# One of three sums of weight blocks moved from VectorE into an accumulating DMA

## The chip, the cores and the metric

The kernel runs on one core of a Trainium2 chip. The metric is the device time of one execution in microseconds; for the kernel before it is the median of three runs.

## The reference, cut to what matters

Two layers, each with a half-step SwiGLU feed-forward block, a parallel token mixer and a second feed-forward block, on 256 tokens of 1024 features. The change touches only the feed-forward blocks:

```python
def _swiglu(h, wg, wu, wd):
    return (jax.nn.silu(h @ wg) * (h @ wu)) @ wd

for l in range(DEPTH):
    f = _swiglu(_rmsnorm(h, ff1_norm_pre[l]), ff1_w_gate[l], ff1_w_up[l], ff1_w_down[l])
    h = h + 0.5 * _rmsnorm(f, ff1_norm_post[l])
    m = _hybrid_mixer(_rmsnorm(h, mix_norm_pre[l]), w_in[l], ...)
    h = h + _rmsnorm(m, mix_norm_post[l])
    f = _swiglu(_rmsnorm(h, ff2_norm_pre[l]), ff2_w_gate[l], ff2_w_up[l], ff2_w_down[l])
    h = h + 0.5 * _rmsnorm(f, ff2_norm_post[l])
```

`wg` and `wu` are 1024 by 2816, `wd` is 2816 by 1024, all float32.

## The kernel before, in words

**Precision.** Each float32 operand is split into two float32r parts: ScalarE copies it into `hi` (line 98 for weights, 199 for activations) and VectorE subtracts to get `lo` (line 99, 200). A product is three matmuls: hi by hi, hi by lo, lo by hi.

**Stages.** There are four feed-forward stages, two mixers between them. In a feed-forward stage the 2816 hidden columns are eleven units of 256. Units 0 and 1 are done first (`ffn_first`, line 307). Then come, in turn, "quads" of two units (blocks 2, 5 and 8, each two units wide) and "pairs" of one unit (4, 7, 10; lines 285 to 287). After each, the down projections of the units before it are added into PSUM accumulators (`mm_rows`, line 322), once for each half of the tokens; in the code such a pair of projections is a `downs` entry.

**A quad** multiplies the 256 by 1024 activations by the 1024 by 512 columns of the gate and of the up weights in one two-by-two block product with seven products in place of eight (Winograd's form of Strassen's). The right factors are the four weight blocks g1, u1, g2, u2 and their sums:

- T1 = g1 + u1
- T2 = g1 + u1 + u2
- T3 = u1 + u2
- T4 = g1 + u1 + u2 + g2

Each factor is 128 partitions by 2048 elements and is used by one product (`product`, line 416: 12 matmuls of 512 columns); four of the factors are sums. The left factors S1 to S4 and X11, X12, X22 are made once for each stage in `pre_turn`. The function `ffn_quad` multiplies T1, g1, T2, T3, g2, T4 and u2 in this order, with the sums of the products on VectorE between them.

**The weight pipeline** (`Weights`). `plan_ffn` lists units (one load of 1 MB each, issued by SyncE, line 77) and jobs (one split each). Four raw buffers hold loaded units; a job frees those it names. Five pairs of split buffers hold `hi` and `lo` until the product that uses them is done. A job can name a sum: VectorE then adds two raw buffers into the job's own raw buffer in two halves (line 97) ahead of the split. `pump` loads and splits as far ahead as the buffers let it.

**What sets the order.** The code gives each instruction a place; a list scheduler at build time may move an instruction ahead of others on its engine when its inputs and its buffer would be ready earlier by the scheduler's own times. On the chip each engine then runs its list in order. So splits, left factors and down projections are interleaved in another order than the code has them.

**GpSimd** has only the power -0.5 of the norms to compute (line 210). Temporary activations of 512 elements live in tag `t`, which has 22 buffers; the mixers use most of them.

Of the kernel before, what the change touches and what calls it, by code (L numbers as in the profile page):

```python
# [13 lines left out]
AF = mybir.ActivationFunctionType  # L14
ALU = mybir.AluOpType
AX = mybir.AxisListType

P = 128
# [10 lines left out]
UNIT = 2048  # L29
# [18 lines left out]
class Weights:  # L48
# [9 lines left out]
        self.units.append((src, cols))  # L58
        return len(self.units) - 1

    def job(self, unit, sum_of=None, free=(), pieces=2):


        self.jobs.append((unit, sum_of, free, pieces))
        return len(self.jobs) - 1

    def plan(self, src, cols=UNIT, pieces=2):
# [17 lines left out]

    def split_next(self):
        i, nc = self.split, self.nc
        u, sum_of, free, pieces = self.jobs[i]
        cols, raw = self.units[u][1], self.raw[u]
        hi = self.splitp.tile([P, KD * QDT], F32R, tag="hi", name=f"hi{i}")  # L90
        lo = self.splitp.tile([P, KD * QDT], F32R, tag="lo", name=f"lo{i}")
        step = cols // pieces
        for c in range(0, cols, step):
            s = slice(c, c + step)
            if sum_of:
                x, op, y = sum_of
                nc.vector.tensor_tensor(raw[:, s], self.raw[x][:, s], self.raw[y][:, s], op=op)  # L97
            nc.scalar.activation(hi[:, s], raw[:, s], AF.Copy)  # L98
            nc.vector.tensor_tensor(lo[:, s], raw[:, s], hi[:, s].bitcast(F32), op=ALU.subtract)  # L99
        for v in free:  # L100
            del self.raw[v]
            self.live -= 1
        self.parts[i] = (hi, lo)
        self.split += 1
        self.held += 1
# [25 lines left out]
def hybrid_trunk_kernel(ctx: ExitStack, tc: tile.TileContext, a, out: bass.AP):  # L131
    nc = tc.nc
# [3 lines left out]
    tmp = ctx.enter_context(tc.tile_pool(name="tmp", bufs=1))  # L136
# [3 lines left out]
    ids = iter(range(10**6))  # L140

    def buf(dtype=F32, n=512, tag="t"):
        return tmp.tile([P, n], dtype, tag=tag, name=f"{tag}{next(ids)}", bufs={"t": 22, "n": 8}[tag])

    def tiny(n):
        return small.tile([P, n], F32, tag=f"s{n}", name=f"s{next(ids)}", bufs=2 if n > 64 else 12)
# [1 line left out]
    def bank(tag="wk"):  # L148
        return psum.tile([P, 512], F32, tag=tag, name=f"{tag}{next(ids)}")
# [4 lines left out]
    W = Weights(nc, rawp, splitp)  # L154
# [20 lines left out]
    ones = tmp.tile([1, P], F32, tag="n", name="ones", bufs=8)  # L175
    nc.vector.memset(ones, 1.0)
    zeros = buf(BF16, 512, "n")
    nc.vector.memset(zeros, 0.0)
    warm = bank()
# [33 lines left out]
    def square_sum(x, n, gain=1.0):  # L213

        junk, ssq = buf(BF16, 512, "n"), tiny(1)
        nc.scalar.activation(junk, x, AF.Square, scale=1.0 / (gain * math.sqrt(n)), accum_out=ssq)  # L216
        return ssq

    def post(t, f, gain, store=None):

        fg = [buf(tag="n"), buf(tag="n")]

        def scaled(i):
            nc.vector.tensor_tensor(fg[i], f[i], gains[:, 1, i * 512 : (i + 1) * 512], op=ALU.mult)

        ssq = [square_sum(f[0], D, gain)]
        scaled(0)
        ssq.append(square_sum(f[1], D, gain))
        r = rsqrt_sum(ssq, EPS / (gain * gain))
        scaled(1)  # L230
        for i in range(2):
            s = slice(i * 512, (i + 1) * 512)
            nc.vector.scalar_tensor_tensor(h[:, t, s], fg[i], r, h[:, t, s], op0=ALU.mult, op1=ALU.add)
            if store:
                store(t, s)
# [90 lines left out]
    def plan_ffn(l, n):  # L326


        p = {}

        def down(i):
            p["d", i] = W.plan(a[f"ff{n}_d"][l, i])

        def pair(i):
            for k in "gu":
                p[k, i] = W.plan(a[f"ff{n}_{k}"][l, PAIRS.index(i)])

        for i in range(2):
            for k in range(2):
                p["f", i, k] = W.plan(a[f"ff{n}_f"][l, 2 * i + k], pieces=4)  # L340
        before = list(FIRST)
        for i in range(2, NU):
            if i in PAIRS:
                pair(i)
                for b in before:
                    down(b)
                before = [i]
            elif i in QUADS:
                src = a[f"ff{n}_q"][l, QUADS.index(i)]
                g1, u1, u2 = (W.unit(src[k]) for k in (0, 1, 3))  # L350
                p["T1", i] = W.job(u1, (g1, ALU.add, u1))
                p["g1", i] = W.job(g1)
                p["T2", i] = W.job(u1, (u1, ALU.add, u2))
                p["T3", i] = W.job(g1, (u1, ALU.subtract, g1), free=(g1,))
                late = i == QUADS[-1]
                if not late:
                    down(before[0])
                g2 = W.unit(src[2])
                p["g2", i] = W.job(g2)
                for b in before[1:]:  # L360
                    down(b)
                p["T4", i] = W.job(u1, (u1, ALU.add, g2), free=(u1, g2))
                p["u2", i] = W.job(u2, free=(u2,))
                if late:
                    down(before[0])
                before = [i, i + 1]
        for b in before:
            down(b)
        return p
# [40 lines left out]
    def product(ps, left, job, first):  # L410

        hi, lo = (w[:, :UNIT].rearrange("p (k n) -> p k n", k=4) for w in W.get(job))
        parts = [(k, i) for k in range(4) for i in range(2)] + [(k, 2) for k in range(4)]
        for n, (k, i) in enumerate(parts):
            x, w = ((left[0], hi), (left[0], lo), (left[1], hi))[i]
            nc.tensor.matmul(ps, x[:, k, :], w[:, k, :], start=first and n == 0, stop=n == len(parts) - 1,  # L416
                             skip_group_check=not first)
        W.done(job)

    def ffn_quad(i, p, left, turn, downs):  # L420


        late = i == QUADS[-1]
        turn(0)
        pc = bank()
        product(pc, left["S1"], p["T1", i], True)
        h1 = buf()
        nc.scalar.activation(h1, pc, AF.Copy)
        pa = bank()
        product(pa, left["X11"], p["g1", i], True)  # L430
        w2 = buf()
        nc.scalar.activation(w2, pa, AF.Copy)
        turn(1)
        W.pump()
        pb = bank()
        product(pb, left["S2"], p["T2", i], True)
        nc.vector.tensor_tensor(w2, pb, w2, op=ALU.add)
        nc.vector.tensor_tensor(pc, pc, w2, op=ALU.subtract)  # L438
        W.pump()
        pd = bank()  # L440
        product(pd, left["S3"], p["T3", i], True)
        nc.vector.tensor_tensor(pd, pd, w2, op=ALU.add)
        nc.vector.tensor_tensor(h1, h1, pd, op=ALU.subtract)
        W.pump()
        if not late:
            downs[0]()
        product(pa, left["X12"], p["g2", i], False)
        h0 = buf()
        nc.scalar.activation(h0, pa, AF.Silu)
        W.pump()  # L450
        for f in downs[1:]:
            f()
        product(pd, left["X22"], p["T4", i], False)
        nc.scalar.activation(w2, pd, AF.Silu)
        nc.vector.tensor_tensor(h1, h1, w2, op=ALU.mult)
        W.pump()
        product(pc, left["S4"], p["u2", i], False)
        nc.vector.tensor_tensor(h0, pc, h0, op=ALU.mult)
        W.pump()
        if late:  # L460
            downs[0]()
        return [h0, h1]

    def ffn(l, n, p, gain, turned, left, next_left, before_next, last, later=None):
# [21 lines left out]
        for i in range(2, NU):  # L486
            if i not in QUADS + PAIRS:
                continue
            if hf:
                for b in before:  # L490
                    hT[b] = (buf(F32R), buf(F32R))

            def turn(t):
                if hf:
                    turn_h(t, hf[t], [hT[b] for b in before])

            if i in PAIRS:
                hT[i] = ffn_pair(i, p, turn)
                for b in before:
                    both(b)  # L500
                hf, before = None, [i]
            else:
                hf = ffn_quad(i, p, left, turn, [lambda b=b: both(b) for b in before])
                before = [i, i + 1]
            if later:
                later()
                later = None
# [408 lines left out]
    for l in range(DEPTH):  # L916
        plans.append((plan_ffn(l, 1), plan_mix(l), plan_ffn(l, 2)))
# [7 lines left out]
    left = {}  # L925
# [13 lines left out]
    for l in range(DEPTH):  # L939
# [17 lines left out]
        left = {}  # L957
        turned = mixer(l, mx, turned, left, step(2))
        left, now = None if end else {}, left
# [99 lines left out]
```

## Time and profile before

| what | value |
|---|---|
| median of three runs | 965.74 us (961.45 to 966.24) |
| the profiled execution | 964.58 us, of which the span is 962.5 us |
| busy TensorE, VectorE, ScalarE, GpSimd | 940.0, 814.6, 584.3, 19.7 us |
| chain that ended last | 77% TensorE, 13% VectorE, 5% ScalarE, 2% DMA |
| mean granted clock of TensorE | 0.991 of full speed |
| moved by DMA | 178.03 MB, a mean of 185 GB/s |

The span is the profiled execution from its first to its last instruction. A busy TensorE is not one at its peak, as its matmuls overlap: the time of a run of matmuls is read from start to start. In the rows, PE is TensorE, PEld its loading of the stationary operand, DVE is VectorE, ACT is ScalarE, POOL is GpSimd and SP is SyncE; L97 is line 97; "out<-in" are tiles by their names without numbers; times are microseconds unless marked ns.

### The profile page before, as it was taken

The numbers are of one execution on the slowest core, as the hardware profiler recorded it, in microseconds if no ns is written. First come the engines' busy times: TensorE is split into PE (matmuls) and PEld (weight loads), VectorE is DVE, ScalarE is ACT, GpSimd is POOL, SyncE is SP. The second block draws the span as 40 slices with busy tenths as digits, with TensorE's granted clock in tenths as the row PEclk, the third lists the DMA queues.
The fourth block names the chain that finished last, engine by engine and source line by source line (L and its number), as shares of the span: only waits on it lengthen the run. The fifth ranks groups of instructions, "written<-read, shape, count | busy, mean of one in ns | idle before, by whom it ended". The sixth has DMA issues, their size and how long they took to land.

```text
span 962.5 us, 13043 instructions
## 1 busy us (share of the span) xinstructions
PE 940.0 (98%) x5064; PEld 800.9 (83%) x5064; DVE 814.6 (85%) x1088; ACT 584.3 (61%) x923; POOL 19.7 (2%) x33
## 2 busy tenths in 40 slices
PE   8999999999999999999999999999999999999997
PEld 5679898988988779898977888898888877979895
DVE  5997899688797989899598989986878798889982
ACT  7665566467656565566466656666584565656651
POOL 0000000010001000000000000000000100000000
PEclk9989999999999999999999999999999999999999
DMA  7464365755243355466642727293733242927241
GB/s 295 186 251 186 144 250 206 277 182 212 88 144 116 109 210 228 158 236 232 249 175 81 295 109 284 95 362 135 268 124 131 88 154 88 345 92 300 93 177 44
DMA packets 26706, 178.03 MB, mean 185 GB/s; under 512 B 2962, under 2 KB 3346, under 8 KB 6292
## 3 DMA queue, kind: packets, MB, share of 16 engines
q1 hardware_dynamic: 26644, 177.19, 49.6%
q8 instruction: 40, 0.66, 0.3%
q14 instruction: 22, 0.18, 0.1%
HBM read 176.13 MB, written 1.05 MB: 184 GB/s over the span
## 4 chain that ended last, share of the span: by engine, by line
PE 77%; DVE 13%; ACT 5%; issue 2%; DMA 2%; POOL 1%; SPq 0%; DVEq 0%; POOLq 0%; ACTq 0%
PE acc L322 25%; PE wk L416 21%; PE wk L286 6%; PE wk L285 6%; PE wk L287 6%; DVE lo L99 6%; PE wk L307 5%; DVE raw L97 3%; ACT hi L98 2%; ACT n L216 1%; PE wk L391 1%; DMA raw<-in_ff_q 1%; DVE n L200 1%; POOL s L210 1%; PE wk L852 1%
## 5 line engine op out<-in xcount | busy, mean ns | idle before, releaser
L98 ACT ACTIVATE hi<-raw 128x1024 fp32r<-128x1024 f32 (+2 forms) x440 | 399.3, 958 | 179.6 <-DVE raw L97 57.6
L99 DVE TENSOR_TENSOR lo<-raw,hi 128x1024 fp32r<-128x1024 f32 (+2 forms) x440 | 466.1, 1100 | 15.7 <-ACT hi L98 14.7
L322 PE MATMUL acc<-hi,t 128*128 128x512 f32 x832 | 238.4, 395 | 3.3 <-DVE t L200 1.4
L322 PEld LDWEIGHTS acc<-hi,t 128*128 128x128 f32 x832 | 154.4, 188 | 38.5 <-ACT t L199 4.5
L285 PE MATMUL wk<-xT,hi 128*128 128x256 f32 x544 | 156.1, 287 | 0.0
L286 PE MATMUL wk<-xT,hi 128*128 128x256 f32 x544 | 154.8, 285 | 0.0
L287 PE MATMUL wk<-xT,lo 128*128 128x256 f32 x544 | 154.7, 284 | 0.0
L322 PE MATMUL acc<-lo,t 128*128 128x512 f32 x416 | 133.0, 391 | 4.1 <-DVE lo L99 4.1
L307 PE MATMUL wk<-hi,xT 128*128 128x512 f32 x384 | 124.4, 399 | 3.8 <-ACT xT L199 2.2
L416 PE MATMUL wk<-hi,n 128*128 128x512 f32 x384 | 126.6, 394 | 0.0
L97 DVE TENSOR_TENSOR raw<-raw,raw 128x1024 f32<-128x1024 f32 x96 | 113.7, 1216 | 2.5 <-DMA raw<-in_ff_q 2.5
L286 PEld LDWEIGHTS wk<-xT,hi 128*128 128x128 f32 x544 | 105.1, 193 | 0.7
L285 PEld LDWEIGHTS wk<-xT,hi 128*128 128x128 f32 x544 | 105.1, 193 | 0.6
L287 PEld LDWEIGHTS wk<-xT,lo 128*128 128x128 f32 x544 | 104.9, 193 | 0.1
L322 PEld LDWEIGHTS acc<-lo,t 128*128 128x128 f32 x416 | 77.7, 188 | 21.9 <-DVE lo L99 5.9
L416 PE MATMUL wk<-hi,xT 128*128 128x512 f32 x288 | 94.6, 389 | 0.0
L307 PEld LDWEIGHTS wk<-hi,xT 128*128 128x128 f32 x384 | 72.9, 191 | 21.4 <-ACT xT L199 3.3
L416 PEld LDWEIGHTS wk<-hi,n 128*128 128x128 f32 x384 | 73.1, 190 | 15.7 <-DVE wk L438 0.2
L307 PE MATMUL wk<-lo,xT 128*128 128x512 f32 x192 | 76.2, 398 | 0.6 <-DVE lo L99 0.6
L416 PE MATMUL wk<-lo,n 128*128 128x512 f32 x192 | 75.8, 395 | 0.0
L416 PEld LDWEIGHTS wk<-hi,xT 128*128 128x128 f32 x288 | 54.1, 188 | 11.6
L199 ACT ACTIVATE t<-wk 128x256 fp32r<-128x256 f32 x72 | 26.9, 378 | 54.7 <-PE wk L391 34.6
(182 smaller groups left out, 840.1 us busy)
## 6 DMA issues: line engine op xcount, KB each, us to landing
raw<-in_ff_q SPq DMA_DIRECT2D x48, 1024.0 KB, 7.1
raw<-in_ff_d SPq DMA_DIRECT2D x44, 1024.0 KB, 7.0
raw<-in_ff_f SPq DMA_DIRECT2D x15, 1024.0 KB, 5.1
raw<-in_ff_g SPq DMA_DIRECT2D x12, 1024.0 KB, 5.3
raw<-in_ff_u SPq DMA_DIRECT2D x12, 1024.0 KB, 4.9
raw<-in_w_in SPq DMA_DIRECT2D x10, 1024.0 KB, 5.6
raw<-in_w_kvz SPq DMA_DIRECT2D x8, 1024.0 KB, 7.0
raw<-in_w_out SPq DMA_DIRECT2D x8, 1024.0 KB, 4.9
```

Of the source, the lines that this page charges most:

```text
L97: nc.vector.tensor_tensor(raw[:, s], self.raw[x][:, s], self.raw[y][:, s], op=op)
L98: nc.scalar.activation(hi[:, s], raw[:, s], AF.Copy)
L99: nc.vector.tensor_tensor(lo[:, s], raw[:, s], hi[:, s].bitcast(F32), op=ALU.subtract)
L199: nc.scalar.activation(hi, src_f32, AF.Copy)
L200: nc.vector.tensor_tensor(lo, src_f32, hi.bitcast(F32), op=ALU.subtract)
L210: nc.gpsimd.tensor_tensor(r, v, halfexp, op=ALU.pow)
L285: nc.tensor.matmul(ps, hi[:, k, s], x[0][:, k, :], start=k == 0, stop=False)
L286: nc.tensor.matmul(ps, hi[:, k, s], x[1][:, k, :], start=False, stop=False)
L287: nc.tensor.matmul(ps, lo[:, k, s], x[0][:, k, :], start=False, stop=k == KD - 1)
L307: nc.tensor.matmul(ps, y[:, k, :], w[:, k, :], start=h == 0 and n == 0, stop=h == 1 and n == len(parts) - 1)
L322: nc.tensor.matmul(acc[b], x[:, j, s], w[:, j, b * 512 : (b + 1) * 512], start=first and j == 0 and i == 0, stop=last and j == 1 and i == 2)
L416: nc.tensor.matmul(ps, x[:, k, :], w[:, k, :], start=first and n == 0, stop=n == len(parts) - 1, skip_group_check=not first)
```

## The change

T3 = u1 + u2 is no longer made by VectorE. When T1 has been split, GpSimd issues a DMA that reads u2's block once more from HBM and adds it into u1's raw buffer, and T3 is split from there. T1, T2 and T4 are still summed by VectorE, now in place in g1's buffer (before: T1, T2 and T4 in u1's, T3 in g1's). So the order of the jobs and of the products is changed too: g1 comes ahead of T1, and T3 comes behind the first down projection, except in the last quad of a stage, where that projection stays at the end. The scratch space for DMA commands grows from 1024 to 4096, and tag `t` has 20 buffers in place of 22.

```diff
-    def job(self, unit, sum_of=None, free=(), pieces=2):
-        self.jobs.append((unit, sum_of, free, pieces))
+    def job(self, unit, sum_of=None, free=(), pieces=2, then=None):
+        self.jobs.append((unit, sum_of, free, pieces, then))
...
             nc.scalar.activation(hi[:, s], raw[:, s], AF.Copy)
             nc.vector.tensor_tensor(lo[:, s], raw[:, s], hi[:, s].bitcast(F32), op=ALU.subtract)
+        if then:
+            nc.gpsimd.dma_start(self.raw[then[0]][:, :UNIT], then[1], accum_op=ALU.add)
...
-    bufs={"t": 22, "n": 8}[tag]
+    bufs={"t": 20, "n": 8}[tag]
...
                 g1, u1, u2 = (W.unit(src[k]) for k in (0, 1, 3))
-                p["T1", i] = W.job(u1, (g1, ALU.add, u1))
                 p["g1", i] = W.job(g1)
-                p["T2", i] = W.job(u1, (u1, ALU.add, u2))
-                p["T3", i] = W.job(g1, (u1, ALU.subtract, g1), free=(g1,))
+                p["T1", i] = W.job(g1, (g1, ALU.add, u1), then=(u1, src[3]))
+                p["T2", i] = W.job(g1, (g1, ALU.add, u2))
                 late = i == QUADS[-1]
                 if not late:
                     down(before[0])
+                p["T3", i] = W.job(u1, free=(u1,))
                 g2 = W.unit(src[2])
                 p["g2", i] = W.job(g2)
...
-                p["T4", i] = W.job(u1, (u1, ALU.add, g2), free=(u1, g2))
+                p["T4", i] = W.job(g1, (g1, ALU.add, g2), free=(g1, g2))
...
         turn(0)
+        pa = bank()
+        product(pa, left["X11"], p["g1", i], True)
+        w2 = buf()
+        nc.scalar.activation(w2, pa, AF.Copy)
         pc = bank()
         product(pc, left["S1"], p["T1", i], True)
         h1 = buf()
         nc.scalar.activation(h1, pc, AF.Copy)
-        pa = bank()
-        product(pa, left["X11"], p["g1", i], True)
-        w2 = buf()
-        nc.scalar.activation(w2, pa, AF.Copy)
         turn(1)
...
         W.pump()
+        if not late:
+            downs[0]()
         pd = bank()
         product(pd, left["S3"], p["T3", i], True)
...
-        if not late:
-            downs[0]()
...
-    dynamic_dma_scratch_size=1024
+    dynamic_dma_scratch_size=4096
```

## Rows read from the trace of the kernel before

**Rows 1.** The page, part 1: busy time, share of the span, instructions

```profile
PE 940.0 (98%) x5064; PEld 800.9 (83%) x5064; DVE 814.6 (85%) x1088; ACT 584.3 (61%) x923; POOL 19.7 (2%) x33
```

**Rows 2.** Windows: stretch, its length, busy time by engine, TensorE's clock, DMA share, GB/s

```profile
45.00:53.00 8.00, 4.49 (x13) 2.69 (x14) 7.13 (x11) 3.79 (x7) 0.00 (x0) 0.83 0.28 92
53.00:58.00 5.00, 5.00 (x15) 3.93 (x14) 3.69 (x5) 2.10 (x3) 0.00 (x0) 0.58 0.66 274
...
340.00:484.00 144.00, 143.74 (x781) 124.80 (x782) 125.00 (x138) 87.27 (x117) 0.55 (x1) 1.00 0.59 219
```

**Rows 3.** Waits of TensorE from 20 to 75 us: total, times, longest

```profile
PE acc L322 <- DVE lo L99: 1.6, 1, 1.6
PE acc L322 <- DVE t L200: 1.4, 1, 1.4
...
PE acc L322 <- ACT t L199: 0.5, 1, 0.5
```

**Rows 4.** Waits of TensorE over the whole span

```profile
PE acc L322 <- DVE lo L99: 4.1, 4, 1.6
PE wk L307 <- ACT xT L199: 2.2, 4, 1.1
...
PE acc L322 <- ACT hi L98: 0.5, 2, 0.2
```

**Rows 5.** Timeline of VectorE in the first start: start, length, instructions

```profile
31.29 2.35 DVE L97 TENSOR_TENSOR raw<-raw,raw 128x1024 f32<-128x1024 f32 x2
...
39.30 3.48 DVE L97 TENSOR_TENSOR raw<-raw,raw 128x1024 f32<-128x1024 f32 x3
...
50.65 0.75 DVE L200 TENSOR_TENSOR t<-wk,t 128x256 fp32r<-128x256 f32 x2
```

**Rows 6.** Groups by line and shape: total and mean ns, then idle time before

```profile
L98 ACT ACTIVATE hi<-raw 128x1024 fp32r<-128x1024 f32 x344 | 344.4, 1052 | 166.9 <-DVE raw L97 57.6 <-PE wk L286 27.6 <-DMA raw<-in_ff_d 23.3
...
L97 DVE TENSOR_TENSOR raw<-raw,raw 128x1024 f32<-128x1024 f32 x96 | 113.7, 1216 | 2.5 <-DMA raw<-in_ff_q 2.5
```

**Rows 7.** Timeline of TensorE: where the first two products end in two starts

```profile
44.31 0.60 PE L391 MATMUL wk<-ident,t 128*128 128x128 f32 x4
...
337.73 0.60 PE L391 MATMUL wk<-ident,t 128*128 128x128 f32 x4
```

**Rows 8.** Chain that ended last, 377 to 446 us: start, length, piece

```profile
387.93 10.88 PE wk L416 x48
...
435.75 10.43 PE wk L416 x46
```

**Rows 9.** Line 210 on GpSimd: shortest, median, longest ns

```profile
L210 POOL TENSOR_TENSOR s<-s,halfexp x28: 548/550/1397, 6.6 to 957.4; 128x1 f32<-128x1 f32 x28
```

**Rows 10.** The page, part 6: loads, count, KB each, median us to landing

```profile
raw<-in_ff_q SPq DMA_DIRECT2D x48, 1024.0 KB, 7.1
...
raw<-in_ff_u SPq DMA_DIRECT2D x12, 1024.0 KB, 4.9
```

**Rows 11.** Windows of 10 us; the third with TensorE alone

```profile
36.00:46.00 10.00, 9.64 (x46) 7.47 (x44) 10.00 (x10) 6.56 (x8) 0.00 (x0) 1.00 0.35 136
...
425.00:435.00 10.00, 10.00 (x46) 8.14 (x45) 10.00 (x12) 5.38 (x7) 0.00 (x0) 1.00 0.01 3
...
820.00:830.00 10.00, 10.00 (x45) 1.00 1.00 378
```

**Rows 12.** Timeline of VectorE at T1's sums of blocks 2, 5 and 8

```profile
316.62 2.35 DVE L97 TENSOR_TENSOR raw<-raw,raw 128x1024 f32<-128x1024 f32 x2
...
372.49 2.35 DVE L97 TENSOR_TENSOR raw<-raw,raw 128x1024 f32<-128x1024 f32 x2
...
420.27 2.35 DVE L97 TENSOR_TENSOR raw<-raw,raw 128x1024 f32<-128x1024 f32 x2
...
436.98 3.48 DVE L99 TENSOR_TENSOR lo<-raw,hi 128x1024 fp32r<-128x1024 f32 x3
```

**Rows 13.** Windows: most of the first mixer

```profile
210.00:300.00 90.00, 89.09 (x552) 77.82 (x551) 69.69 (x146) 52.61 (x111) 2.49 (x3) 0.96 0.43 151
```

More of the change, by code (lines that the diff above doesn't have):

```diff
@@ L87, in split_next @@
         i, nc = self.split, self.nc
-        u, sum_of, free, pieces = self.jobs[i]
+        u, sum_of, free, pieces, then = self.jobs[i]
         cols, raw = self.units[u][1], self.raw[u]
@@ L142, in buf @@
     def buf(dtype=F32, n=512, tag="t"):
-        return tmp.tile([P, n], dtype, tag=tag, name=f"{tag}{next(ids)}", bufs={"t": 22, "n": 8}[tag])
+        return tmp.tile([P, n], dtype, tag=tag, name=f"{tag}{next(ids)}", bufs={"t": 20, "n": 8}[tag])
     def tiny(n):
@@ L1046 @@
     from concourse.bass_utils import run_bass_kernel_spmd as _run
-    nc = _bacc.Bacc("TRN2", target_bir_lowering=False, num_devices=1, dynamic_dma_scratch_size=1024)
+    nc = _bacc.Bacc("TRN2", target_bir_lowering=False, num_devices=1, dynamic_dma_scratch_size=4096)
     arrays, aps = {}, {}
```

## The prediction

> **What bounds the kernel now.** I read the page first: TensorE is busy 940.0 of 962.5 us [rows 1]; the chain that ended last is for the most part its matmuls. The change leaves TensorE's work as it is, so the room is what TensorE does not use: some 22 us, and the time in which its clock is down. Second, the table of windows shows where that is. In the steady part of a feed-forward stage (340 to 484 us) TensorE is busy 143.74 of 144 us at a granted clock of 1.00, while VectorE has 13% idle [rows 2]: there the change can cost, but not gain. The room lies at the starts of the four feed-forward stages, and the first is the largest: from 45 to 53 us TensorE is busy 4.49 of 8 us, and until 58 us its clock is partly at the lower level [rows 2].
>
> Third, the waits of TensorE. In the first start it waits 1.6 us for a `lo` of the weight splits, and 1.4 and 0.5 us for the split of the hidden activations, 3.5 together [rows 3]. Over the whole span the wait for `lo` is 4.1 us in four places, one at each start, so 2.5 us are left for the three later ones, and 0.5 us for `hi` beside it [rows 4]. Fourth, VectorE's timeline of the first start says why: from 31.29 to 51 us it works without a pause, and sums stand ahead of the splits that TensorE waits for (three in a row at 39.30) [rows 5].
>
> **The change part by part.** *Removed:* T3's sum, two VectorE instructions in each of 12 blocks, 24 of the 96 on line 97. One takes 1.216 us with its tail [rows 6]; in a row they come 1.13 us apart (three end within 3.48 us, [rows 5]), so 2.27 us a block and 27 us in all. In the steady parts this buys nothing, since TensorE ends last there.
>
> *At the first start.* VectorE's row from 31.29 to 50.65 us holds six sums and ten splits, with two products of 0.6 us between. Without two sums it ends 2.3 us sooner. As T3 also moves behind the first down projection, that projection's own two splits move up by T3's two as well: 4.5 us in all, from 50.65 to about 46.1 at the latest. TensorE ends the first two products at 44.31 us [rows 7] and then has T2 to do, 2.72 us (one product of 12 matmuls, a fourth of 10.88, [rows 8]). A shift of 2.3 us leaves 1.2 of the 3.5 us of waits, one of 4.5 none; I take 2.9 back.
> The clock: at the full rate of 46 matmuls in 10 us [rows 11], the 15 matmuls in the 5 us from 53 would take 3.3 us, and the 13 in the 4.49 busy microseconds before them 2.8; so the lower clock, 0.83 and 0.58 in these windows, costs 1.7 + 1.7 = 3.4 us [rows 2]. It fell after TensorE had paused. With little pause left I take 2.1 back. Together -5.0 (bounds 0 and -6.9).
>
> *At the three later starts* the wait is for the same splits, and 2.3 to 4.5 us cover it: -2.5, and -0.3 of the 0.5 for `hi`, so -2.8 (bounds 0 and -3.0).
>
> *The order of the first two products:* g1 needs no sum, so it can be split while T1 still needs one; but T1 and T2 are now summed in g1's buffer, one behind the other. The count of VectorE and ScalarE instructions is the same, and VectorE's row was without gaps anyway: 0.
>
> *Added: 12 accumulating loads of 1024 KB, issued by GpSimd.* They pass no work in SyncE's queue. GpSimd otherwise computes 28 powers, 0.55 us each in the median and 1.4 at most [rows 9], all in norms. A load that waits for T1's sums has no power behind it before the stage's end (at the starts, those of the norms before come first), so the wait on GpSimd costs 0. Behind the load waits ScalarE's `hi` of T3, and behind that, in order, ScalarE's evictions and VectorE's `lo`.
> No row shows such a load. Lower bound: a plain load of the same size, 4.9 us from issue to landing in the fastest group [rows 10]. Upper bound: three passes (source, old contents, result) of the 7.1 us that the same source tensor's loads take [rows 10], 21.3 us. Nearest is the plain load of that tensor, with one more pass for the old contents at 378 GB/s, the rate of a window in which DMA was fully busy [rows 11], 2.8 us: I take 7.1 + 2.8 = 9.9 us. The Trainium skill (Collectives: The Full Stack, "The bandwidth ceiling: the fold count and why AG ≠ RS ≠ AR") says that an adding DMA issues two source reads per chunk and so runs at half the rate of a copy; by it two passes alone, at 378 GB/s, make 5.5 us as an estimate, every block would be met all the more, and the sum would stay. No run shows it yet.
>
> How long it may take, from the end of T1's sums to 2.2 us before T3's first matmul (one `hi` of 1.05 us and one `lo` of half a tile, [rows 6]), with g1's two splits (2.27 us) now ahead of T1's sums:
> - First start: sums end at about 36.4. TensorE reaches T3 at 44.3 + 0.6 + 2.7 + 5.4 (first down projection, two halves) = 53.0. Allowed 14.4 us.
> - Later starts: sums began at 316.62 [rows 12] and would end at 321.2; the first two products end at 337.73 [rows 7], so T3 comes at 346.5. Allowed 23 us.
> - Second block of a stage (block 5): sums began at 372.49 [rows 12] and would end at 377.0; products start at 387.93 [rows 8], T3 after three products (8.16) and a projection (5.44), at 401.5. Allowed 22 us.
> - Last block (block 8), in which no projection stands ahead of T3: sums began at 420.27 [rows 12] and would end at 424.8; products start at 435.75 [rows 8], T3 at 443.9. Allowed 16.9 us.
>
> At 9.9 us all are met, and the cost is 0. What hides it is the lookahead of five split buffers. The DMA engines have room where the loads fall, since the four raw buffers are full then: their share is 0.01 from 425 to 435 us [rows 11]. Where the cover is gone, each late microsecond is paid once in each of the four last blocks. The raw buffer of u1 comes free one job later, that of the projection one job sooner: 0.
>
> *Two buffers fewer* of tag `t` (22 to 20) touch the mixers. No row shows a wait for a buffer by name; from 210 to 300 us TensorE is busy 89.09 of 90, and VectorE has 20 us idle [rows 13]. Bounds 0, and 3 us for each of two mixers; near the lower end, +0.7. For DMA traffic, 12 MB more at 378 GB/s are 33 us of transfer, nearly all behind the lookahead: bounds 0 and 3, and I add +0.5.
>
> *Sum:* -5.0 - 2.8 + 0.7 + 0.5 = -6.6 us on the profiled execution's 964.58 (span 962.5 and 2.1 around it), so 958.0. The median of the runs is 1.2 us above that execution; against it I forecast 959.
>
> **The rivals.**
> 1. *The gain stays small.* The first accumulating load is issued near 36.4 us, when DMA is still at work on earlier loads: a share of 0.35 from 36 to 46 us [rows 11]. With 3 to 5 us of queueing, T3's wait takes the place of the one removed, TensorE pauses again, and the clock falls as before. For it: 14.4 us is the tightest allowance. Against it: most of that window is free. Then the first start gives 0 to -1, and the time is 964.58 - 2.8 - 0.5 + 1.2 = 962.5, against the median 963.5 to 964.
> 2. *Slower: the accumulating load is slow.* Place: the last block of each stage, where T3 follows T2 at once. Price: beyond 16.9 us, 4 us per microsecond, and in the first start one more beyond 14.4. It outweighs the 6.6 us from about 17.7 us a load (5L - 82 = 6.6). At 20 us: 12.4 + 5.6 - 6.6 = +11.4, so 976, against the median 977; at the upper bound 21.3 us, 984. For it: nothing here shows the adding rate, and ScalarE's queue stops at T3's `hi`. Against it: one load has all 16 DMA engines almost for itself.
> 3. *GpSimd can't start the load while VectorE works.* In the last block VectorE is busy without a pause from 420.27 until past 440 us [rows 12]. If the load started only then, T3 would come at 440.4 + 9.9 + 2.2 = 452.5 in place of 443.9: 8.6 us late, 34 us over four stages, about 993. The Trainium skill (SBUF — State Buffer, "SBUF: two separate sides") warns of this for loads issued from GpSimd; it names the two-port modes of VectorE, and says under "Who interferes with whom" that an operation on two tensors has none. Nearly all of VectorE's time here is such operations, so I give it little.
>
> **How the numbers follow.** About 0.5%, 4.8 us, is what a measurement of this kernel can tell from no change. The forecast (its own range 953 to 961) has 0.48; rival 1 has 0.30; rival 2 has 0.18; rival 3 has 0.04. Faster is the forecast, and 0.02 of rival 1 at its best: 0.50. The same is the rest of rival 1: 0.28. Slower is rivals 2 and 3: 0.22. The range goes from 953 (the bounds of the gains, -9.9, and the waits for activations at the starts, 2.2 us [rows 4], gone too) to 979, rival 2 with a load of just over 20 us; outside stay rival 3 and the top of rival 2.
>
> **What would show it.** VectorE has 72 sums on line 97 in place of 96, and is busy some 29 us less. The new load takes 8 to 12 us from issue to landing. From 45 to 58 us TensorE has no wait of over 1 us, and its clock stays at 1.00. T3's `hi` never waits for DMA where TensorE waits too. The steady parts keep their lengths to within 1 us. Wrong would be: TensorE waiting for T3 in last blocks (the load takes over 17 us); a pause and a low clock between 45 and 60 us as before; or new waits in the mixers, above all for activations kept in tag `t`.

## The result, and the profile after

The changed kernel takes 958.55 us, the median of 7 runs (958.22 to 960.75), beside 965.74 us for the kernel before (961.45 to 967.83, 7 runs): a ratio of 0.9936, interval 0.9917 to 0.9956. The forecast was 959. A second set of runs, beside a later experiment, gave 958.80 and a ratio of 0.9931 (0.9915 to 0.9947). The span of the profiled execution fell from 962.5 to 956.6 us.

The page after, its parts 1, 3 and 6: busy time by engine, then queues with packets, megabytes and share of the 16 DMA engines, then loads with their count, size and median from issue to landing:

```profile
PE 937.3 (98%) x5064; PEld 797.5 (83%) x5064; DVE 789.6 (83%) x1064; ACT 580.4 (61%) x923; POOL 32.6 (3%) x45
...
q1 hardware_dynamic: 26644, 177.19, 51.0%
q0 software_dynamic: 1728, 12.58, 7.2%
...
raw<-in_ff_q SPq DMA_DIRECT2D x48, 1024.0 KB, 5.1
...
raw<-in_ff_q POOLq DMA_DIRECT2D x12, 1024.0 KB, 8.1
```

Beside [rows 1], VectorE has 24 instructions and 25.0 us less (T3's is one of four sums of a block, not of three as the title has it: 24 of 96); TensorE has as many matmuls as before. An accumulating load lands 8.1 us after its issue in the median, 3.0 us later than a plain load of the same tensor in this kernel. The landing times of the twelve accumulating loads:

```profile
DMA to landing us min/median/max: 7.8/8.1/9.3
```

The windows that stood in [rows 2], and the waits of TensorE, first from 20 to 75 us, then the largest of the whole span:

```profile
45.00:53.00 8.00, 6.56 (x29) 4.61 (x28) 5.67 (x9) 4.05 (x9) 0.00 (x0) 1.00 0.63 194
53.00:58.00 5.00, 5.00 (x24) 4.14 (x23) 5.00 (x5) 4.53 (x5) 0.00 (x0) 1.00 0.32 134
340.00:484.00 144.00, 144.00 (x784) 124.41 (x784) 120.20 (x136) 87.79 (x123) 3.15 (x4) 1.00 0.67 227
```

```profile
PE acc L325 <- ACT t L202: 1.3, 1, 1.3
PE wk L310 <- DVE lo L100: 0.6, 1, 0.6
PE wk L310 <- ACT hi L99: 0.3, 1, 0.3
...
PE acc L325 <- DVE t L203: 3.2, 3, 1.1
PE wk L254 <- DVE n L245: 2.7, 1, 2.7
PE wk L184 <- DVE n L181: 1.3, 1, 1.3
```

From 45 to 58 us, taken as one window, TensorE now has 51 matmuls where it had 26, at a clock of 1.00 throughout. The steady part is as full as before, 784 matmuls for 781. The wait for `lo` in the accumulations is gone; in its place stand one wait for ScalarE (1.3 us) in the first start and one for VectorE's `t`, up to 1.1 us, in each of the three later ones.

Where the time went, from the first products of `ffn_first` or of a block to the next landmark in the timelines of TensorE:

| stretch | before, us | after, us | difference, us |
|---|---|---|---|
| first start, to the first pair | 65.64 | 60.14 | -5.50 |
| the three later starts, each to the first pair | 56.17, 56.18, 56.26 | 55.61, 55.58, 55.60 | -1.82 in all |
| block 5 and its pair in the last stage | 48.96 | 47.95 | -1.01 |
| end of the second and third stage | 32.35, 35.37 | 32.85, 35.83 | +0.96 in all |
| the two mixers, each from its first matmuls of 256 columns to the products of `z` | 43.35, 40.38 | 40.38, 43.39 | +0.04 in all |

These add up to -7.3; before the first start +0.66 is lost, at the last stage's end some 0.4, and the rest is tenths in other blocks, which gives the 5.9 by which the span is shorter. Two lines are not the change's: the mixers' (see the last section) and block 5's. A kernel like the one before but with 20 buffers (below) has 47.77 in place of 48.96 there, and 64.44 in place of 65.64 in the first start, so the old order scatters by 1.2 us in both. The changed kernel's second profile has 60.48 in the first start: its gain is 4.0 to 5.5 us.

VectorE's and ScalarE's timelines of the first start after (start, length, instruction; in brackets the idle time and what ended it):

```profile
34.63 2.35 DVE L98 TENSOR_TENSOR raw<-raw,raw 128x1024 f32<-128x1024 f32 x2
...
39.85 2.35 DVE L98 TENSOR_TENSOR raw<-raw,raw 128x1024 f32<-128x1024 f32 x2
...
42.45 4.62 DVE L100 TENSOR_TENSOR lo<-raw,hi 128x1024 fp32r<-128x1024 f32 x4
48.12 2.36 DVE L100 TENSOR_TENSOR lo<-raw,hi 128x1024 fp32r<-128x1024 f32 x2 [1.05 <-ACT hi L99]
```

```profile
47.03 2.01 ACT L99 ACTIVATE hi<-raw 128x1024 fp32r<-128x1024 f32 x2 [1.96 <-DMA raw<-in_ff_q]
48.94 0.64 ACT L202 ACTIVATE t<-wk 128x256 fp32r<-128x256 f32 x2
```

The three sums in a row [rows 5] are gone, and four `lo` follow the second pair of sums at once. The load is issued at 37.60 us, and T3's `hi` starts 9.43 us later, so this is the slowest of the twelve; the `hi` waits 1.96 us for it, ScalarE's evictions stand behind that `hi`, and at 49.63 us TensorE has waited 1.31 us for one of them.

### The profile page after: what moved, and what is told of

Its sections match the earlier page's. It is cut to its first block, busy times and chain, and to the rows that moved or that the text cites. A ratio compares the mean times of both kernels' runs of the same rounds, so it can differ in the third digit from the quotient of the medians.

```text
span 956.6 us, 13144 instructions
## 1 busy us (share of the span) xinstructions
PE 937.3 (98%) x5064; PEld 797.5 (83%) x5064; DVE 789.6 (83%) x1064; ACT 580.4 (61%) x923; POOL 32.6 (3%) x45
## 3 DMA queue, kind: packets, MB, share of 16 engines
q1 hardware_dynamic: 26644, 177.19, 51.0%
q0 software_dynamic: 1728, 12.58, 7.2%
## 4 chain that ended last, share of the span: by engine, by line
PE 79%; DVE 9%; ACT 5%; issue 4%; DMA 2%; POOL 1%; SPq 0%; POOLq 0%; DVEq 0%; ACTq 0%
PE acc L325 25%; PE wk L419 22%; PE wk L289 7%; PE wk L288 7%; PE wk L290 7%; DVE lo L100 4%; PE wk L310 4%; ACT hi L99 2%; DVE raw L98 1%; ACT n L219 1%; POOL s L213 1%; PE wk L394 1%; DMA raw<-in_ff_q 1%; DVE n L203 1%; PE wk L855 1%
## 5 line engine op out<-in xcount | busy, mean ns | idle before, releaser
L98 DVE TENSOR_TENSOR raw<-raw,raw 128x1024 f32<-128x1024 f32 x72 | 86.2, 1217 | 1.3 <-DMA raw<-in_ff_q 0.9
L310 PE MATMUL wk<-lo,xT 128*128 128x512 f32 x192 | 76.0, 397 | 0.6 <-DVE lo L100 0.6
L419 PE MATMUL wk<-lo,xT 128*128 128x512 f32 x144 | 56.2, 390 | 0.0
```

The lines of the kernel that those rows point to most:

```text
L310: nc.tensor.matmul(ps, y[:, k, :], w[:, k, :], start=h == 0 and n == 0, stop=h == 1 and n == len(parts) - 1)
```

## The experiments

**The new order without the load.** T3 keeps its new place, and VectorE makes its sum.

```diff
-                p["T1", i] = W.job(g1, (g1, ALU.add, u1), then=(u1, src[3]))
+                p["T1", i] = W.job(g1, (g1, ALU.add, u1))
-                p["T3", i] = W.job(u1, free=(u1,))
+                p["T3", i] = W.job(u1, (u1, ALU.add, u2), free=(u1,))
```

> The new order of jobs and products, with 20 buffers of tag t, but T3 summed by VectorE in u1's buffer (u1 + u2); no accumulating load. Theory A (the gain comes from VectorE's two sums a block that are gone): VectorE has 96 sums again, TensorE pauses 1 to 3 us near 45 to 52 us and its clock falls there, and the time is 962 to 966 us. Rival B (the gain comes from the order: the first projection's splits no longer stand behind T3's): by the prediction's own working those splits are ready at 46.1 us with the sum as without it, and T3's by 50.7 us, ahead of the 53 us at which TensorE needs it; then the first start is as short as with the load and the time is 957 to 960 us.

Measured: 967.59 us, ratio 1.0029 (1.0015 to 1.0044): nothing gained, a little lost. VectorE's timeline of its first start:

```profile
34.23 3.48 DVE L98 TENSOR_TENSOR raw<-raw,raw 128x1024 f32<-128x1024 f32 x3
...
40.50 3.49 DVE L98 TENSOR_TENSOR raw<-raw,raw 128x1024 f32<-128x1024 f32 x3
43.91 6.89 DVE L100 TENSOR_TENSOR lo<-raw,hi 128x1024 fp32r<-128x1024 f32 x6
```

The code has T3's sum behind the first projection's splits, but the list scheduler put both halves of it ahead: six sums stand before the six `lo`, TensorE waits 2.0 us for `lo` and 1.9 us for `t`, and its clock is 0.74 from 45 to 58 us. The first start takes 64.70 us, as in the old order. The later starts lose too (+2.35, +0.74 and +0.66 us; of the first of these some 1.7 is a clock of 0.83 from 340 to 350 us). The profiled execution is the longest of the twelve, 972.0 us at a mean clock of 0.986; the others took 965.28 to 969.31 us at 0.993 to 0.995. The order of VectorE's list is the same in all of them, the clock is not. Where the other eleven lose against the changed kernel, at nearly its clock, is not shown.

**The load without the new place of T3.** T3's job and product stand ahead of the first projection, as before the change.

```diff
                 p["T2", i] = W.job(g1, (g1, ALU.add, u2))
+                p["T3", i] = W.job(u1, free=(u1,))
...
-        if not late:
-            downs[0]()
         pd = bank()
         product(pd, left["S3"], p["T3", i], True)
...
         W.pump()
+        if not late:
+            downs[0]()
```

> The accumulating load is kept, but T3's job and product stand ahead of the first down projection again, as in the kernel before. Theory A: VectorE's two sums are gone all the same, so most of the gain stays, 958 to 961 us. Rival B: T3's split waits for the load, which lands near 46 us, and the projection's splits stand behind it on ScalarE and VectorE; TensorE waits 2 us or more near 45 to 53 us, its clock falls, and the time is 962 to 967 us. In the middle blocks T3 comes 5.4 us sooner, which the allowance of 22 us covers: nothing to see there.

Measured: 966.45 us, ratio 1.0013 (1.0001 to 1.0025). The waits from 40 to 60 us, of all engines, and two windows:

```profile
ACT hi L99 <- DMA raw<-in_ff_q: 5.7, 2, 4.2
...
PE acc L325 <- ACT hi L99: 5.0, 1, 5.0
```

```profile
45.00:53.00 8.00, 2.70 (x8) 1.55 (x7) 5.55 (x5) 6.36 (x9) 0.00 (x0) 0.64 0.18 38
53.00:58.00 5.00, 5.00 (x22) 4.02 (x21) 3.62 (x7) 2.40 (x3) 0.00 (x0) 0.89 0.92 377
```

ScalarE's list has T3's `hi` ahead of the projection's, waits for the load with the projection's weights at hand, and TensorE waits 5.0 us. The first start gains nothing (+0.3), the later ones 0.5 to 0.6 us each, as in the changed kernel. So neither half of the change pays alone in the whole time.

**Twenty buffers in the kernel before.** Only the count of tag `t` and the scratch space are the changed kernel's.

```diff
-    bufs={"t": 22, "n": 8}[tag]
+    bufs={"t": 20, "n": 8}[tag]
...
-    nc = _bacc.Bacc("TRN2", target_bir_lowering=False, num_devices=1, dynamic_dma_scratch_size=1024)
+    nc = _bacc.Bacc("TRN2", target_bir_lowering=False, num_devices=1, dynamic_dma_scratch_size=4096)
```

> The kernel before with 20 in place of 22 buffers of tag t and the larger scratch, nothing else. The prediction put +0.7 us on this (bounds 0 and 6). If the buffers matter, ScalarE or VectorE waits anew in the mixers and the time is 967 us or more; if not, it is that of the kernel before to within 1 us.

Measured: 964.92 us, ratio 0.9999 (0.9983 to 1.0015). The two buffers cost nothing that can be measured (the interval is 1.5 us to either side).

**The load in block 2 alone.** Blocks 5 and 8 keep the new order and let VectorE make T3's sum.

```diff
-                p["T1", i] = W.job(g1, (g1, ALU.add, u1), then=(u1, src[3]))
+                p["T1", i] = W.job(g1, (g1, ALU.add, u1), then=(u1, src[3]) if i == QUADS[0] else None)
-                p["T3", i] = W.job(u1, free=(u1,))
+                p["T3", i] = W.job(u1, None if i == QUADS[0] else (u1, ALU.add, u2), free=(u1,))
```

> The changed kernel with the accumulating load in block 2 of each stage alone; blocks 5 and 8 sum T3 on VectorE, in the new order. Theory: in the steady parts TensorE ends last, so the eight loads that are gone bought nothing, and the time is that of the changed kernel, 957 to 960 us. Rival: VectorE's sums in blocks 5 and 8 count after all (its lookahead shrinks), and the time is 961 us or more.

Measured: 959.87 us, ratio 0.9947 (0.9927 to 0.9967). The first start is 60.48 us long, the later ones 55.6: all of the gain is there with four of the twelve loads. The other eight save 16 sums on VectorE and buy nothing that the two medians, 1.3 us apart, can show.

**The load in two halves** of 512 KB, each by an instruction of its own.

```diff
-            nc.gpsimd.dma_start(self.raw[then[0]][:, :UNIT], then[1], accum_op=ALU.add)
+            for c in range(0, UNIT, UNIT // 2):
+                s = slice(c, c + UNIT // 2)
+                nc.gpsimd.dma_start(self.raw[then[0]][:, s], then[1][:, s], accum_op=ALU.add)
```

> The accumulating load is issued as two of 512 KB, so that the first half of T3 can be split before the second half has landed. Theory: in the first start ScalarE's wait for the load (2.0 us) and the 1.3 us for which TensorE waits behind it shrink to near nothing; 0.5 to 1.5 us less than the changed kernel, 957 to 958.5 us. Rival: each half costs GpSimd's whole issue (0.87 us) and its own latency, and the sum lands no sooner: the same as the changed kernel.

Measured: 959.80 us, ratio 0.9951 (0.9932 to 0.9970), as the changed kernel. In the trace TensorE's wait for ScalarE's `t` in the first start goes from 1.3 to 0.3 us, and that start is 59.01 us long: the load is what T3's `hi` waited for. One microsecond does not show in the medians.

**The load issued twice.** T3 becomes u1 + 2 u2, which changes the values and no other work.

```diff
             nc.gpsimd.dma_start(self.raw[then[0]][:, :UNIT], then[1], accum_op=ALU.add)
+            nc.gpsimd.dma_start(self.raw[then[0]][:, :UNIT], then[1], accum_op=ALU.add)
```

> The accumulating load is issued twice, the second behind the first, so T3 becomes u1 + 2 u2 (the output is another one). It makes T3 ready some 16 to 17 us after T1's sums in place of 8.1. By the prediction's allowances (14.4 us in the first start, 16.9 in the last block of a stage, 22 and 23 elsewhere) T3 comes 2 to 3 us late in the first start and is just in time in the last blocks: 960 to 966 us. If the cover were thinner than worked out (ScalarE stops at T3's split, and what stands behind it is late too), each of twelve blocks pays several us and the time is 975 us or more; if thicker, it stays at 959.

Measured: 992.31 us, ratio 1.0287 (1.0267 to 1.0307). The largest waits of its TensorE, and ScalarE's timeline in the first start:

```profile
PE wk L420 <- DVE t L449: 10.6, 8, 3.0
PE wk L420 <- DVE t L204: 8.7, 1, 8.7
PE acc L326 <- ACT t L203: 6.4, 3, 2.7
```

```profile
58.21 2.00 ACT L99 ACTIVATE hi<-raw 128x1024 fp32r<-128x1024 f32 x2 [12.02 <-DMA raw<-in_ff_q]
60.12 0.58 ACT L436 ACTIVATE t<-wk 128x512 f32<-128x512 f32 x1
60.60 0.37 ACT L203 ACTIVATE t<-wk 128x256 fp32r<-128x256 f32 x1
```

From the first issue at 37.51 us T3 is ready for its split after 20.7 us here; elsewhere the second load is issued 8.2 us behind the first, so two take about 16.4. That is inside the allowances of blocks 2, 5 and 8 in the later stages (23, 22, 16.9 us), yet every stage loses: of 34 us some 15 in the first, 5 to 6 in each later one, and 3 in the mixers, where the clock fell for longer. TensorE's largest waits are not for T3's splits: no `hi` or `lo` is among these rows. ScalarE stands before T3's `hi` for 12.02 us with evictions and splits of turned activations behind it, and TensorE waits for such (6.4 and 8.7 us) and for VectorE's subtraction after T3's product (line 449, 10.6 us). In all, ScalarE's waits at a `hi` for a load of this tensor grow from 8.8 us in the changed kernel to 86.4. The cover of the load is far thinner than it was priced.

**The sum on VectorE, held behind the splits.** No load. A factor 1 is made by VectorE from the last `lo` of the job before, and T3's sum multiplies by it, so that the scheduler can't move the sum ahead. The sum costs 1.28 us in place of 1.22.

```diff
+            one = self.splitp.tile([P, 1], F32, tag="one", name=f"one{i}")
+            nc.vector.tensor_scalar(one, self.last[:, UNIT - 1 : UNIT].bitcast(F32), 0.0, 1.0, op0=ALU.mult, op1=ALU.add)
...
-                nc.vector.tensor_tensor(raw[:, s], self.raw[x][:, s], self.raw[y][:, s], op=op)
+                    nc.vector.scalar_tensor_tensor(raw[:, s], self.raw[x][:, s], one, self.raw[y][:, s], op0=ALU.mult, op1=op)
```

> The new order, no accumulating load, T3 summed by VectorE as in e1, but its sum reads a factor 1 that VectorE computes from the job before it, so that the scheduler can't place the sum ahead of that job's splits. Theory C (e1 lost because the scheduler put T3's sums ahead of the splits of T1, T2 and the projection; the load's worth is that it takes the sum out of VectorE's list): the projection's splits are ready at about 46 us in the first start, TensorE waits under 1.5 us there, and the first pair starts near 72 us as in the changed kernel; the time is 957 to 961 us although VectorE has 96 sums. Rival A (VectorE's time itself): the first start stays long (the pair near 76 us) and the time is 963 to 968 us.

Measured: 969.14 us, ratio 1.0047 (1.0033 to 1.0060). But its first start is as short as with the load. The windows, and VectorE's timeline:

```profile
45.00:53.00 8.00, 8.00 (x38) 6.46 (x37) 8.00 (x11) 5.16 (x9) 0.00 (x0) 1.00 0.36 131
```

```profile
43.23 4.62 DVE L106 TENSOR_TENSOR lo<-raw,hi 128x1024 fp32r<-128x1024 f32 x4
...
48.49 2.47 DVE L102 SCALAR_TENSOR_TENSOR raw<-raw,one,raw 128x1024 f32<-128x1024 f32 x2
```

TensorE is busy all 8 us at full clock, and the second pair starts 4.58 us earlier than before (4.92 in the changed kernel; the first pair stands elsewhere in this kernel's order). So at the first start it is the order on VectorE's list that pays, not VectorE's 25 us. What it loses comes later: block 5 with its pair takes 48.7 us in place of 47.9, block 8 with its pair 46.1 in place of 45.4, in every stage. No wait of TensorE is listed there. Its matmuls of 512 columns are slower in this kernel, not there alone but in all of it; the same groups in the changed kernel and here:

```profile
L325 PE MATMUL acc<-hi,t 128*128 128x512 f32 x832 | 238.3, 395 | 4.5 <-DVE t L203 3.2
L419 PE MATMUL wk<-hi,n 128*128 128x512 f32 x384 | 125.2, 390 | 0.1
```

```profile
L330 PE MATMUL acc<-hi,t 128*128 128x512 f32 x832 | 242.3, 399 | 0.0
L424 PE MATMUL wk<-hi,n 128*128 128x512 f32 x384 | 127.2, 395 | 3.0 <-DVE t L208 3.0
```

At the end of the first mixer, which the edit leaves alone, the first group takes 402 ns in place of 397; the matmuls of 256 columns keep theirs (288 ns on the first of their lines in both). Over all groups of 512 columns the differences of the means add up to some 11 us (an estimate: each times its count), and the span is 10.4 us longer than that of the changed kernel. That VectorE sums T3 in blocks 5 and 8 is not enough as a cause: with the load in block 2 alone it does so too, and there block 5 with its pair takes 47.9 to 48.0 us in three stages and 48.6 in one, block 8 with its pair 45.2 to 45.4. Why the matmuls are slower in this kernel is not shown.

**The sum on GpSimd.** The same two halves, issued by GpSimd in place of VectorE.

```diff
-                nc.vector.tensor_tensor(raw[:, s], self.raw[x][:, s], self.raw[y][:, s], op=op)
+                (nc.gpsimd if then else nc.vector).tensor_tensor(raw[:, s], self.raw[x][:, s], self.raw[y][:, s], op=op)
```

> T3 = u1 + u2 is summed by GpSimd's own arithmetic in place of the accumulating load; all else as in the changed kernel. It takes the sum out of VectorE's list too, without the 12 MB. Theory C: if GpSimd needs under 14 us for the two halves and does not slow VectorE, the time is that of the changed kernel, 957 to 961 us. Rival: GpSimd's two-input sums and VectorE's get in each other's way, lines 98 and 100 take longer than 1.22 us a piece, and the time is 965 us or more.

Measured: 1005.62 us, ratio 1.0419 (1.0397 to 1.0440). GpSimd's group, VectorE's `lo`, and two of these `lo` in the timeline:

```profile
L98 POOL TENSOR_TENSOR raw<-raw,raw 128x1024 f32<-128x1024 f32 x24 | 77.1, 3234 | 389.6 <-DVE raw L98 247.9 <-DVE t L201 141.6
```

```profile
L100 DVE TENSOR_TENSOR lo<-raw,hi 128x1024 fp32r<-128x1024 f32 (+2 forms) x440 | 501.5, 1177 | 68.3 <-ACT hi L99 67.5
```

```profile
36.67 6.68 DVE L100 TENSOR_TENSOR lo<-raw,hi 128x1024 fp32r<-128x1024 f32 x2
```

A sum takes GpSimd 3.23 us, and two `lo` beside it took 6.68 us where they take 2.36 without. GpSimd computing is no free engine here; GpSimd issuing a load cost nothing that was seen.

**Block 2 as changed, blocks 5 and 8 as before.** The load in halves in block 2; the old jobs, products and sums in the others. The changed kernel ran beside it once more.

```diff
+                loaded = i == QUADS[0]
+                if loaded:
                     p["g1", i] = W.job(g1)
                     p["T1", i] = W.job(g1, (g1, ALU.add, u1), then=(u1, src[3]))
                     p["T2", i] = W.job(g1, (g1, ALU.add, u2))
+                else:
+                    p["T1", i] = W.job(u1, (g1, ALU.add, u1))
+                    p["g1", i] = W.job(g1)
+                    p["T2", i] = W.job(u1, (u1, ALU.add, u2))
+                    p["T3", i] = W.job(g1, (u1, ALU.subtract, g1), free=(g1,))
```

> Block 2 of each stage as in the changed kernel, its accumulating load in two halves of 512 KB; blocks 5 and 8 as in the kernel before, jobs and products in the old order, all sums on VectorE. Theory A (the gain is made in block 2 alone, and the new order of the last block costs the 0.45 us that each stage end lost): first start 5 us shorter, later starts 0.6 us each, stage ends no loss; 1.5 to 2 us below the changed kernel, so 956.5 to 957.5. Rival: the stage ends lose 0.45 us here too, or blocks 5 and 8 lose 1 us in the last stage, where the changed kernel gained: then 958.5 to 960, as the changed kernel.

> The changed kernel once more, beside the mixed one on the same chip: 958 to 960 by every theory.

Measured: 958.12 us, ratio 0.9918 (0.9901 to 0.9936), beside 958.80 for the changed kernel: the intervals overlap, and no version is shown to be better than the changed kernel. The stage ends have 32.85 and 35.83 us here too, so the order of the last block doesn't cause their loss; the rival had that right. The trace shows where it lies, though. ScalarE's timeline at the end of the second stage, before and then after the change:

```profile
482.12 0.63 ACT L216 ACTIVATE n<-h 128x512 bf16<-128x512 f32 x1
482.65 0.19 ACT L216 ACTIVATION_READ_ACCUMULATOR n<-h 128x1 f32 x1
482.78 0.63 ACT L216 ACTIVATE n<-h 128x512 bf16<-128x512 f32 x1
```

```profile
474.00 0.63 ACT L219 ACTIVATE n<-h 128x512 bf16<-128x512 f32 x1 [0.26 <-DVE h L236]
474.54 0.19 ACT L219 ACTIVATION_READ_ACCUMULATOR n<-h 128x1 f32 x1
474.63 0.62 ACT L99 ACTIVATE hi<-raw 128x512 fp32r<-128x512 f32 x1
475.15 0.61 ACT L219 ACTIVATE n<-h 128x512 bf16<-128x512 f32 x1
```

The list scheduler set a `hi` of the next weights between the two squares of a norm that TensorE will wait for: half a microsecond a stage, far from the lines of the change. The new order without the load and the load in block 2 alone have this `hi` in the same place. That this one instruction is the whole of the 0.45 us was read, not tried.

## Why the prediction was right, point by point

**What bounds the kernel** held. TensorE's steady parts kept their pace, so VectorE's lighter load bought nothing there (the load in block 2 alone is as good as in all three), and the gain lies at the starts.

**The first start** was the main term, -5.0 with bounds 0 and -6.9; it came to -4.0 to -5.5. Its two parts were off in opposite ways: the waits of the accumulations fell from 3.5 to 1.3 us, by 2.2 where I forecast 2.9 (the 0.6 and 0.3 us on line 310 lie in `ffn_first`, and the 0.6 stood there before too), and the clock stayed at 1.00 where I had let it give back 2.1 of 3.4. Together that is 5.6 us, and the table has 5.5. Of what was to be seen there, "no wait of over 1 us" was wrong by 0.3, "clock at 1.00" right. Wrong in kind was the sentence that T3's `hi` never waits for DMA where TensorE waits too: it waits 1.96 us, and TensorE 1.31 behind it.

**Why it pays** was put as less work on VectorE and an earlier place of the projection's splits. The runs sharpen this: the new place alone is undone by the scheduler (967.59), the load alone makes ScalarE wait at T3's `hi` (966.45), and a sum held in its place shortens the first start as much as the load does. The load's worth there is that no sum of T3 is left on VectorE's list to be moved ahead. Whether a held sum would match the load in the whole time too stays open, as that variant's matmuls are slower throughout. The clock follows the pause: in this start it fell in the four profiles in which TensorE paused there much as before or longer (the kernel before, the same with 20 buffers, and each half of the change alone), and it stayed at 1.00 in both profiles of the changed kernel and in the four variants whose first start is short.

**The later starts** were mis-sized: -1.8 for -2.8. The wait for `lo` went, as forecast, but six `lo` now stand in a row on VectorE ahead of the splits of turned activations; its timeline at the second stage's start and TensorE's:

```profile
326.04 6.89 DVE L100 TENSOR_TENSOR lo<-raw,hi 128x1024 fp32r<-128x1024 f32 x6
332.85 1.29 DVE L203 TENSOR_TENSOR t<-wk,t 128x256 fp32r<-128x256 f32 x3
```

```profile
333.31 1.19 PE L325 MATMUL acc<-hi,t 128*128 128x512 f32 x4 [1.06 <-DVE t L203]
```

I asked what T3's move takes away from the projection's splits, and not what is late next behind those six.

**The load** took 8.1 us for 9.9 forecast, between plain (5.1) and my sum. The cost of 0 held to within the 1.3 us above. The Trainium skill (Collectives: The Full Stack, "The bandwidth ceiling: the fold count and why AG ≠ RS ≠ AR") says of the reduce step of a ring collective that its add needs two source reads and so runs at half the rate of a copy. The profile's page agrees for this load: 7.2% of the span for 12.58 MB is 0.57% per MB, and 51.0% for 177.19 MB is 0.29%, a factor of 2.0. But the second figure holds transfers of all sizes, and no run issues a plain load from GpSimd, so how much of the factor is the adding is not shown; from issue to landing it is 1.6 (8.1 to 5.1 us). The allowances were the weak step: "14.4, 23, 22, 16.9" counted until T3's own product, but ScalarE's list stops at T3's `hi`, and other work that TensorE needs stands behind it. With two loads that cost 34 us, where those allowances charge 6.3 in the first start (20.7 less 14.4) and nothing at the 16.4 us elsewhere. So rival 2's mechanism is real; it starts below the 17.7 us that I gave as its point, and the load was short enough to stay clear of it.

**The rest.** VectorE fell by 25.0 us, not 29: the sums fell by 27.5 ([rows 6], 113.7 to 86.2), and `lo` took 2.6 more. The two buffers, +0.7, cost nothing. DMA traffic, +0.5, is not seen apart from the stage ends' half microseconds, which no step foresaw. The sum said -6.6, the profiled executions differ by 5.9; that these are so near is in part luck. The 1.0 us that block 5 seems to gain is scatter of the old order, and it offsets half of the 2.0 us that no term foresaw (the stage ends, and 0.66 before the first start).

**The rivals.** Rival 1 needed a load delayed by DMA at work; the first load is the slowest of the twelve and does arrive 1.96 us late for ScalarE, but the clock did not fall. Rival 3 fell: the loads land in 8.1 us in the median though VectorE works, and its timeline in the first start has no pause while the load is under way, other than for the load's own result.

## What to carry to other kernels

Where a list scheduler sets the order, moving an operation off an engine may pay because it leaves the list, and a move in the code alone may be undone: read the built order of the engine before pricing it. When an operation is handed to a DMA, count the cover to the first instruction that stands behind its consumer on any in-order engine, not to the product that uses it. Then try it in the one place where the bounding engine waits; here four of twelve loads made the whole gain.

## What the runs showed of the hardware that was not expected

The stretch of a mixer in the table above takes 40.38, about 41.9 or about 43.35 us, whatever the kernel: before has 43.35 and 40.38, after 40.38 and 43.39, and the changed kernel's second profile 41.93 and 41.90. Windows of the first mixer, before and after (the same work lies some 5 us earlier in the second):

```profile
235.00:240.00 5.00, 5.00 (x20) 2.76 (x18) 2.22 (x6) 2.19 (x7) 0.00 (x0) 0.81 0.46 187
240.00:245.00 5.00, 5.00 (x24) 4.67 (x24) 4.42 (x13) 2.31 (x10) 0.00 (x0) 0.51 0.00 0
```

```profile
230.00:235.00 5.00, 5.00 (x23) 2.92 (x24) 2.62 (x7) 2.58 (x9) 0.00 (x0) 1.00 0.48 197
235.00:240.00 5.00, 5.00 (x45) 5.00 (x44) 5.00 (x14) 4.31 (x15) 0.00 (x0) 1.00 0.01 3
```

TensorE's clock falls in this stretch in some executions and not in others, for 0, 1.5 or 3.0 us a mixer. That is as much as most terms of this forecast, and of the order of the runs' own spread. Why it falls or not stays open; without the mixers the two spans differ by 5.9 us too (962.5 less 83.73, 956.6 less 83.77).

The other surprise is that one variant, the sum held behind the splits, has slower matmuls of 512 columns all through the kernel, also where its edit changes nothing and the granted clock is 1.00. Nothing in its trace tells why.
